# Output projection of the HGRN mixer as seven products on half matrices, product by product, with the operand sums on GpSimd

## The chip, the cores and the metric

The kernel runs on one core of one Trainium2 chip. The metric is device time in microseconds (us) of one execution, the median of repeated runs. A core has five engines that each work through their own instruction stream in order and wait for each other through semaphores: TensorE (PE: matrix multiplication; its weight loads are shown as PEld), VectorE (DVE), ScalarE (ACT), GpSimd (POOL) and SyncE (SP), which here does nothing but issue DMA transfers. GpSimd issues some DMA transfers too. A stream in order means that an instruction that waits holds up everything behind it on its engine.

## The reference

One layer of an encoder trunk over 1024 positions with a model width of 1024. Only the part around the changed product matters here:

```python
def _token_mixers(h, ...):
    proj = jnp.einsum("bsd,de->bse", h, w_in)
    glu_in, q, v, z_f, z_b, og, g_a, g_b = jnp.split(proj, SPLIT_POINTS, axis=-1)
    ...
    a = jax.nn.silu(_layernorm(a, ln_w, ln_b))
    a = jnp.einsum("bsc,cd->bsd", a, pw_w)
    o = _bi_hgrn2(q, v, z_f, z_b, lb[0], lb[1])
    ...
    bmix = (of * jax.nn.silu(og.astype(jnp.float32))).astype(h.dtype)
    bmix = jnp.einsum("bse,ed->bsd", bmix, o_w)
    return jax.nn.sigmoid(g_a) * a + jax.nn.sigmoid(g_b) * bmix
```

The line with `o_w` is the o projection: the 1024 x 1024 result of the eight heads (128 channels each) times a 1024 x 1024 weight. Its result is gated and added to the convolution branch, and the sum goes into `w_out`, the next product. After that comes the feed-forward part (`ffn_w_up`, `ffn_w_down`).

## The kernel before

Everything lies with channels on the 128 partitions and positions along the free axis, in two halves of 512 positions. A tile of 128 x 512 (called a page) is the unit of nearly all work. Every fp32 product is made of three matmuls (`mm3`, lines 149 to 151): weight and operand are each split into a rounded high part and a remainder (`split`, line 125: ScalarE casts the high part, then VectorE subtracts it from the source for the low part), and high x high, high x low and low x high are added up in PSUM. So one 128 x 128 block of weights against one half costs three 128x128 by 128x512 matmuls.

The stages run one after the other on TensorE: the input projections (those of large columns in pairs, `s_pairs`, by seven products on half matrices already); from about 362 to 470 us, in the midst of these pairs, the depthwise convolution's normalisation (`conv_norm`, a LayerNorm across partitions, from line 1086 on); the scan of the eight heads; the pointwise product of the convolution branch; the o projection from 867.7 us; `w_out` from 954.9 us; then the feed-forward part.

In `conv_norm`, TensorE has two small pieces of work for each half. `all_rows` (line 591) sums the four column tiles over partitions after the DVE line 1096, and `rstd_over_partitions` (line 602) does the same for the squares after the DVE line 1107. Both stand at fixed places between the matmuls of the projections, on TensorE's in-order stream. The DVE lines of the chain (1091, 1096, 1102, 1107) are pinned with `pin`, so they stay in program order with the other pinned rows.

A head's result is transposed at the end of its scan (line 1460), gated on DVE (line 1462) and stored to DRAM as `d_bm[h][half]`; head seven, the last, is split right away and stays in SBUF. `bm_loads(half)` loads the other seven heads of a half into pages `A` and splits them. The o projection itself is `o_jobs`: eight column tiles `i` of 128 output columns; for each, both halves; for each, eight heads `k`, three matmuls each: 8 x 2 x 8 x 3 = 384 matmuls. The weights come as eight loads of 512 KB (`raw_w`, two pages `wr`), each split into `wp` pages by ACT and DVE. `merge(i)` multiplies an accumulator with the gate `d_gb`, adds the convolution branch `d_a` (both loaded by SP) and splits the sum into the `mg` pages, the operands of `w_out`.

While the o projection runs, `weight_sums` (lines 1602 to 1620) prepares sums of the feed-forward part's first weights: 12 loads into eight pages called `h7`, 12 additions on DVE, 12 stores to `d_us`.

What sets the order: each engine's stream is in order. Tiles come from pools with a fixed number of pages (`ev` 3, `tm` 4, `wr` 2, `wp` 4, `h7` 8), and a page's next load waits for the last reader of its previous content. `Stream.fill(n)` emits n pieces of a product; `later(n, do)` puts a chore in a list that is run n pieces on. A scheduler orders unpinned instructions of different engines by what they depend on.

## Time and profile before

| | |
|---|---|
| median of 3 runs | 1706.88 us (1706.85 to 1707.17) |
| the profiled execution | 1706.98 us |
| its span on the core | 1705.0 us |
| PE busy | 1688.6 us (99%) |
| DVE busy | 1269.3 us (74%) |
| ACT busy | 827.3 us (49%) |
| POOL busy | 245.9 us (14%) |
| first matmul of the o projection / of `w_out` | 867.73 / 954.9 us |
| POOL busy from 860 to 955 us | 0 |
| DMA, mean over the span | 180 GB/s |

The span is what the profiler records between the first and the last instruction; 1.98 us of the profiled execution lie around it. Busy time of PE counts matmuls whose modelled ends overlap the next one, so the start-to-start distance is the honest price of a matmul. In rows of the trace, "out<-in" are tile names without buffer numbers, "x3" counts instructions, and a bracket at the end of a row tells how long the engine sat idle before it and what ended that.

### The profile page before, as it was taken

What the parts mean: (1) busy time and instruction counts of PE and PEld (TensorE: products, weight loads), DVE (VectorE), ACT (ScalarE), POOL (GpSimd) and SP (SyncE); (2) the same over time, 40 slices, a digit from 0 to 9 for tenths busy, and PEclk for the clock granted to TensorE, in tenths of its full rate; (3) what the DMA queues carried; (4) which work ended last, traced back from release to release, by engine and by line L of the source; (5) the groups of instructions that cost most, each with busy time, mean ns of one, the idle gap of its engine ahead of it and who ended that gap; (6) DMA issues with size and microseconds to landing.
All of it is one profiled execution on the core that took longest, in us unless ns stands there. A gap on an engine that the chain in (4) does not pass through costs nothing.

```text
span 1705.0 us, 30406 instructions
## 1 busy us (share of the span) xinstructions
PE 1688.6 (99%) x11719; PEld 1408.2 (83%) x11719; DVE 1269.3 (74%) x1938; ACT 827.3 (49%) x1562; POOL 245.9 (14%) x287
## 2 busy tenths in 40 slices
PE   9999999999999999999999999999999999999998
PEld 6788888888888888888888888888888888888787
DVE  5889899887678888888565467676777776657865
ACT  7454343335476777776432345444344434442334
POOL 1312222200001111111100003122222222000110
PEclk9999999999999999999999999999999999999999
DMA  7887887866573444436797455686777776773842
GB/s 240 284 213 186 191 196 172 205 187 206 165 236 100 139 129 134 129 116 221 241 294 243 128 167 176 153 171 143 172 164 178 164 183 149 237 260 102 212 98 99
DMA packets 332871, 306.17 MB, mean 180 GB/s; under 512 B 17454, under 2 KB 244918, under 8 KB 332726
## 3 DMA queue, kind: packets, MB, share of 16 engines
q1 hardware_dynamic: 285366, 265.42, 48.8%
q0 software_dynamic: 47360, 38.81, 15.4%
q8 instruction: 92, 1.51, 0.4%
q14 instruction: 53, 0.43, 0.1%
HBM read 201.40 MB, written 84.93 MB: 168 GB/s over the span
## 4 chain that ended last, share of the span: by engine, by line
PE 70%; ACT 1%; DVE 1%; DMA 0%; issue 0%; POOL 0%; POOLq 0%; ACTq 0%; DVEq 0%
PE mm L149 16%; PE mm L151 16%; PE mm L150 16%; PE sc L149 3%; PE sc L150 3%; PE sc L151 3%; PE ob L1433 2%; PE tr L149 2%; PE tr L150 2%; PE tr L151 2%; PE sc L1247 1%; PE sc L1333 1%; PE mm L1392 1%; PE sc L1392 1%; PE ob L1247 1%; PE tr L1382 0%
## 5 line engine op out<-in xcount | busy, mean ns | idle before, releaser
L149 PE MATMUL mm<-hx,wp 128*128 128x512 f32 x1068 | 425.7, 399 | 0.0
L151 PE MATMUL mm<-hx,wp 128*128 128x512 f32 x1068 | 417.0, 390 | 0.5 <-DVE wp L125 0.5
L150 PE MATMUL mm<-hx,wp 128*128 128x512 f32 x1068 | 416.2, 390 | 0.6 <-POOL hx L125 0.6
L125 ACT CAST wp<-wr 128x1024 fp32r<-128x1024 f32 (+2 forms) x146 | 146.9, 1006 | 224.3 <-PE mm L150 165.0
L151 PEld LDWEIGHTS mm<-hx,wp 128*128 128x128 f32 x1068 | 200.5, 188 | 44.6 <-DVE wp L125 1.6
L149 PEld LDWEIGHTS mm<-hx,wp 128*128 128x128 f32 x1068 | 200.6, 188 | 40.6 <-ACT wp L125 0.2
L150 PEld LDWEIGHTS mm<-hx,wp 128*128 128x128 f32 x1068 | 200.8, 188 | 39.9 <-POOL hx L125 1.0
L125 DVE TENSOR_TENSOR wp<-wr,wp 128x1024 fp32r<-128x1024 f32 (+2 forms) x144 | 169.5, 1177 | 39.8 <-ACT wp L125 39.4
L1065 DVE SCALAR_TENSOR_TENSOR acc<-gl,v_b,acc 128x1024 f32<-128x1024 f32 x120 | 153.5, 1280 | 1.7
L441 ACT COPY su<-mm 128x512 f32<-128x512 f32 x82 | 47.8, 583 | 84.4 <-PE mm L151 84.3
L1371 POOL DMA_DIRECT2D S<-D x64 | 36.1, 571 | 281.1 <-ACT jk L1438 125.3
L125 ACT CAST wq<-sw 128x1024 fp32r<-128x1024 f32 x41 | 43.2, 1054 | 61.3 <-PE mm L150 32.9
L1194 DVE TENSOR_TENSOR qF<-qF,tb 128x512 f32<-128x512 f32 x96 | 65.9, 686 | 9.5 <-ACT A L1228 8.9
L149 PE MATMUL tr<-hx,wp 128*128 128x512 f32 x180 | 70.1, 390 | 0.0
L151 PE MATMUL tr<-hx,wp 128*128 128x512 f32 x180 | 70.1, 389 | 0.0
L150 PE MATMUL tr<-hx,wp 128*128 128x512 f32 x180 | 70.0, 389 | 0.0
L1194 DVE TENSOR_TENSOR kG<-kG,tb 128x512 f32<-128x512 f32 x96 | 65.9, 687 | 4.0 <-ACT A L1228 2.2
L1710 DVE SCALAR_TENSOR_TENSOR tm<-gp,v_a,tm 128x512 f32<-128x512 f32 x88 | 66.0, 750 | 3.3 <-ACT tm L1708 1.3
L302 POOL DMA_DIRECT2D sw<-in_ffn_w_up_dram x38 | 49.8, 1502 | 116.0 <-DMA sw<-in_ffn_w_up_dram 72.4
L149 PE MATMUL sc<-hy,wq 128*128 128x512 f32 x164 | 63.9, 390 | 0.0
L151 PE MATMUL mm<-hy,wp 128*128 128x512 f32 x164 | 63.8, 389 | 0.0
L149 PE MATMUL mm<-hy,wp 128*128 128x512 f32 x164 | 63.8, 389 | 0.0
(377 smaller groups left out, 3721.9 us busy)
## 6 DMA issues: line engine op xcount, KB each, us to landing
wr<-in_w_in_dram SPq DMA_DIRECT2D x48, 512.0 KB, 5.6
wr<-in_ffn_w_up_dram SPq DMA_DIRECT2D x22, 512.0 KB, 5.6
sw<-in_w_in_dram SPq DMA_DIRECT2D x38, 256.0 KB, 3.1
d_g<-ft SPq DMA_DIRECT2D x38, 256.0 KB, 2.0
sw<-in_ffn_w_up_dram SPq DMA_DIRECT2D x38, 256.0 KB, 3.2
sw<-in_ffn_w_up_dram POOLq DMA_DIRECT2D x38, 256.0 KB, 6.7
wr<-sw POOLq DMA_DIRECT2D x32, 256.0 KB, 3.2
wr<-wr POOLq DMA_DIRECT2D x32, 256.0 KB, 3.3
```

Of the source, the lines that this page charges most:

```text
L125: parts = A.copy(hi, src), eng.tensor_tensor(lo, src, hi.bitcast(F32), op=ALU.subtract)
L149: T.matmul(acc, whi[:, k, :], ahi, start=first, stop=False, skip_group_check=again)
L150: T.matmul(acc, whi[:, k, :], alo, start=False, stop=False, skip_group_check=again)
L151: T.matmul(acc, wlo[:, k, :], ahi, start=False, stop=last, skip_group_check=again)
L302: G.dma_start(o, a, accum_op=ALU.add)
L441: A.copy(t, acc)
L1065: V.scalar_tensor_tensor(acc, g[:, k : k + S], tap(k), acc, op0=ALU.mult, op1=ALU.add)
L1194: return V.tensor_tensor(o, a, b, op=op)
L1247: T.matmul(b[g, o], A_t[:, at : at + 32], Q_t(at), start=True, stop=True)
L1371: G.dma_start(S_t[g : g + 32, :, g : g + 32], D_t[g : g + 32])
L1392: T.matmul(u[:, sl], kTs[d][:, sl], v[:, c, :], start=True, stop=True)
L1710: V.scalar_tensor_tensor(c, g[:, o + k : o + k + H], vec("fdw", k * NF + j), c, op0=ALU.mult, op1=ALU.add,)
```

## The change

The o projection becomes seven products on half matrices (Winograd's form of Strassen's scheme, as the input pairs do it). The output columns form four pairs `p` (column tiles `p` and `p + 4`), the heads form four pairs `k` (`k` and `k + 4`), and the positions their two halves. Seven products per pair `p`, four `k` each, three matmuls each: 7 x 4 x 4 x 3 = 336 matmuls. They go product by product over all pairs: 1 for p = 0 to 3, 2 for p = 0 to 3, 6 for p = 0 to 3, then 7 and 4 in turn for each p, then 5 and 3. Products 1, 2 and 4 use weights as they are, 7, 5, 6 and 3 use sums of weights; products 1, 2 and 3 use the heads' halves as they are, 7, 5, 6 and 4 use sums of them.

The sums of weights (`o_sums`) are made in the convolution's norm: eight chores of four loads, four DVE additions of 128x256 and a store to `d_os`, in pages `gl` of the convolution. The sums of operands (`operands`) are made between scan and product: 16 loads of `d_bm` into the eight `h7` pages, 12 additions on GpSimd for k = 0, 1, 2 and four on DVE for k = 3. Operand `b_o[2][3]`, which is half 0 of head seven, is split from the page `d_bm[7][0]` of k = 3; head seven goes through DRAM like the others. Four more loads (`later(28 + 2 * k, ...)`) serve product 3.

The merge multiplies by the gate on DVE (for products 2, 4 and 5 after an addition with a second accumulator, which ACT has copied to SBUF in some cases), and the convolution branch is then added by an accumulating DMA that GpSimd issues. The weights come in 14 groups of two products, 512 KB each. The feed-forward weights' sums are now emitted by the code of the stage behind, `s_out`.

```diff
-            if h == NH - 1:
-                bm[h][half] = split(hx(), hx(), bt, V)
-            else:
-                nc.sync.dma_start(d_bm[h][half], bt)
+            nc.sync.dma_start(d_bm[h][half], bt)
...
+    def o_sums(n):
+        p, ks = n // 2, slice(n % 2 * 2, n % 2 * 2 + 2)
+        t = gp0.tile([P, 4, 2, P], F32, tag="gl", name=nm("os"), bufs=NCW)
+        r, o = o_cols(p)
+        for q, (src, k0) in enumerate(((r, 0), (o, 0), (o, NK2), (r, NK2))):
+            nc.sync.dma_start(t[:, q], src[:, k0 + ks.start : k0 + ks.stop])
+
+        def add():
+            for a, b in ((0, 1), (1, 2), (2, 0), (3, 2)):
+                pin(V.tensor_tensor(t[:, a], t[:, a], t[:, b], op=ALU.add))
+            nc.sync.dma_start(d_os[p].rearrange("p q (k e) -> p q k e", e=P)[:, :, ks], t)
+
+        later(O_LATE, add)
...
     for half in range(2):
+        for n in range(half * ND // 2, half * ND // 2 + ND // 2):
+            later(1 + O_STEP * (n % (ND // 2)), lambda n=n: o_sums(n))
         for pieces in conv_norm(half):
             s_pairs.fill(pieces)
...
+    def merge(e, p, half, x0, x1=None, op=None):
+        i = p + e * NK2
+        t = next(gates_of)()
+        nc.sync.dma_start(t, d_gb[i][half])
+        if x1 is not None:
+            both = x0
+            if e + half < 2:
+                both = page(p4, "x2", 2)
+                A.copy(both, x0)
+            V.tensor_tensor(both, both, x1, op=op)
+            x0 = both
+        V.tensor_tensor(t, x0, t, op=ALU.mult)
+        G.dma_start(t, d_a[i][half], accum_op=ALU.add)
+        mg[i][half] = split(mg_page(), mg_page(), t, V)
...
+    def h7_page(src):
+        t = page(fw, "h7", 2 * NK2)
+        nc.sync.dma_start(t, src)
+        return t
...
+    def operands(k):
+        eng = V if k == NK2 - 1 else G
+        b11, b12, b22, b21 = [
+            h7_page(d_bm[k + h * NK2][half]) for h, half in ((0, 0), (0, 1), (1, 1), (1, 0))
+        ]
+        if k == NK2 - 1:
+            operand(2, k, b21)
+        for i, o, a, b, op in (
+            (7, b22, b12, b22, ALU.subtract),
+            (5, b12, b11, b12, ALU.subtract),
+            (6, b11, b22, b11, ALU.subtract),
+            (4, b21, b11, b21, ALU.add),
+        ):
+            eng.tensor_tensor(o, a, b, op=op)
+            operand(i, k, o)
...
+    o_items = [(i, p) for i in (1, 2, 6) for p in range(NK2)]
+    o_items += [(i, p) for p in range(NK2) for i in (7, 4)]
+    o_items += [(i, p) for i in (5, 3) for p in range(NK2)]
+    o_groups = [o_items[n : n + 2] for n in range(0, len(o_items), 2)]
...
+    for n, d in enumerate(d_us):
+        later(5, weight_sums(*up_cols(n), ND // 2, d))
+        s_out.fill(5)
```

Three places show how instructions move. The same code has higher line numbers in the changed kernel (line 1107 becomes 1129, 602 becomes 610, 149 to 151 become 150 to 152, 125 becomes 126).

The first place is SyncE's stream (SP) at the end of the scan, where the o projection's loads begin. Before, these rows stand there (`d_a` are stores of the convolution branch, `tm` and `ev` the merge's loads, `wr` weights of the o projection, `h7` feed-forward weights):

```order
L1157 DMA d_a_6_1_153<-ev_1703_10533 128x512
L1157 DMA d_a_7_1_155<-ev_1705_10550 128x512
L1575 DMA tm_1762_10780<-d_a_1_1_143 128x512
L1575 DMA ev_1741_10657<-d_gb_0_0_172 128x512
L136 DMA wr_1765_10789<-in_hgrn_o_w_dram 128x8x128
L1608 DMA h7_1746_10692<-in_ffn_w_up_dram 128x4x128
```

In the changed kernel the stream has the store of head seven's second half, the last store of `d_a`, and then 16 loads of `d_bm` into the eight `h7` pages; shown are the first three, the eighth, and the last two with the row behind them:

```order
L1487 DMA d_bm_7_1_283<-ev_1713_10640 128x512
L1181 DMA d_a_7_1_155<-ev_1711_10631 128x512
L1613 DMA h7_1730_10666<-d_bm_0_0_268 128x512
L1613 DMA h7_1731_10668<-d_bm_0_1_269 128x512
L1613 DMA h7_1732_10670<-d_bm_4_1_277 128x512
...
L1613 DMA h7_1741_10696<-d_bm_5_0_278 128x512
...
L1613 DMA h7_1756_10742<-d_bm_7_1_283 128x512
L1613 DMA h7_1757_10744<-d_bm_7_0_282 128x512
L1663 DMA wr_1771_10783<-in_hgrn_o_w_dram 128x4x128
```

The load of `d_bm_7_0` is the sixteenth of the sixteen, and its page is the one that `h7_1741` had, the eighth: with eight pages, the sixteenth load takes the eighth page again.

The second place is TensorE's and DVE's o projection. On TensorE the first tile of product 2 (`tr_1782`) ends with the operand `hx_1758`, `hx_1759`, which is the high and the low part of that page; they are the operands of the twentieth group of three matmuls of the projection (sixteen of product 1, then the fourth of product 2):

```order
L150 MATMUL tr_1782_10852<-hx_1703_10585,wp_1774_10812 128x512
L151 MATMUL tr_1782_10852<-hx_1704_10586,wp_1774_10812 128x512
L152 MATMUL tr_1782_10852<-hx_1703_10585,wp_1775_10813 128x512
L150 MATMUL tr_1782_10852<-hx_1758_10746,wp_1774_10812 128x512
L151 MATMUL tr_1782_10852<-hx_1759_10747,wp_1774_10812 128x512
L152 MATMUL tr_1782_10852<-hx_1758_10746,wp_1775_10813 128x512
L150 MATMUL ob_1787_10876<-hx_1697_10573,wp_1774_10812 128x512
```

Before, TensorE went on through all eight heads of one column tile, and no `h7` page was an operand; this is the head of that row of matmuls:

```order
L1460 MATMUL tr_1727_10596<-ident_68,tm_1649_10337 128x128 x4
L149 MATMUL mm_1740_10632<-hx_1677_10465,wp_1732_10616 128x512
L150 MATMUL mm_1740_10632<-hx_1678_10466,wp_1732_10616 128x512
L151 MATMUL mm_1740_10632<-hx_1677_10465,wp_1733_10617 128x512
L149 MATMUL mm_1740_10632<-hx_1680_10471,wp_1732_10616 128x512
```

On GpSimd the twelve sums stand in one row; the last of the first eight writes `h7_1741`, and the split of it on DVE (`mg_1717`) is its last reader. What moved: the operand of the first tile of product 2 now hangs on a page behind eight sums.

The third place is DVE in the convolution's norm, first half, ahead of the third line 1107 (after which TensorE's line 602 runs). Before:

```order
L1107 TENSOR_TENSOR tm_567_3682<-tm_567_3682,tm_568_3691 128x512
L1107 TENSOR_TENSOR tm_567_3682<-tm_567_3682,tm_570_3702 128x512
L828 TENSOR_TENSOR ev_573_3729<-su_572_3713,mm_548_3609 128x512
L1107 TENSOR_TENSOR tm_567_3682<-tm_567_3682,tm_571_3711 128x512
L125 TENSOR_TENSOR wq_562_3662<-sw_556_3647,wq_561_3661 128x1024
L828 TENSOR_TENSOR ev_581_3769<-sc_550_3611,su_569_3693 128x512
```

In the changed kernel (line 1107 is 1129, 828 is 836, `os` are the pages of `o_sums`):

```order
L836 TENSOR_TENSOR ev_577_3768<-su_576_3752,mm_550_3628 128x512
L1129 TENSOR_TENSOR tm_570_3711<-tm_570_3711,tm_574_3741 128x512
L126 TENSOR_TENSOR wq_565_3691<-sw_559_3676,wq_564_3690 128x1024
L1094 TENSOR_TENSOR os_571_3719<-os_571_3719 128x256
L836 TENSOR_TENSOR ev_585_3813<-sc_552_3630,su_573_3727 128x512
L126 TENSOR_TENSOR wq_568_3698<-w4_563_3688,wq_568_3698 128x512
L1094 TENSOR_TENSOR os_571_3719<-os_571_3719 128x256 x3
L1129 TENSOR_TENSOR tm_570_3711<-tm_570_3711,tm_575_3750 128x512
```

The third line 1129 now stands behind the row of line 836 that reads the accumulator `sc_552`, a split and the additions of line 1094. In the second half it stands, in the same way, behind a split, four additions and two rows of line 299 (298 before); before, the split alone stood between it and the second line 1107, one of the two rows of line 298 stood further ahead and the other behind it.

105 lines of the change are left out of this document (73 added, 32 removed).

## The prediction

> **What bounds the kernel now.** I read the page's first part, then the busy time by stretches, then the timeline of each engine around the places that the change touches.
>
> ```profile
> PE 1688.6 (99%) x11719; PEld 1408.2 (83%) x11719; DVE 1269.3 (74%) x1938; ACT 827.3 (49%) x1562; POOL 245.9 (14%) x287
> ```
>
> TensorE has 16.4 us without work in 1705.0 us. So a matmul that goes away is worth its full pitch, and a wait that TensorE does not have now is paid in full. The stage of the o projection, by stretches (PE, PEld, DVE, ACT and POOL busy, then the granted clock, the DMA share and GB/s):
>
> ```profile
> 870.00:880.00 10.00, 10.00 (x46) 8.29 (x45) 7.00 (x11) 1.77 (x4) 0.00 (x0) 1.00 0.98 305
> 880.00:900.00 20.00, 20.00 (x90) 16.57 (x89) 15.09 (x22) 4.49 (x6) 0.00 (x0) 1.00 0.92 300
> 920.00:940.00 20.00, 20.00 (x90) 16.53 (x89) 9.46 (x13) 3.97 (x5) 0.00 (x0) 1.00 0.61 195
> ```
>
> TensorE never waits here, at the full clock. DVE is busy for three quarters of the time at first, ScalarE for a fifth, GpSimd for nothing, and the DMA engines are nearly full. So GpSimd has room for sums, and what can hurt is a latency: something that arrives late at TensorE's in-order stream.
>
> **What the matmuls are worth.** The pitch is read from the product behind, where 384 matmuls follow each other without a gap:
>
> ```profile
> L149 PE MATMUL mm<-mg,wp x128: 389/389/389, 954.9 to 1041.3; 128*128 128x512 f32 x128
> L151 PE MATMUL mm<-mg,wp x128: 389/389/389, 955.4 to 1041.8; 128*128 128x512 f32 x128
> ```
>
> From the first start (954.9) to the last (1041.8) are 383 steps in 86.9 us, 0.2269 us each (the 389 ns overlap). The change takes 384 matmuls to 336: 48 x 0.2269 = **10.9 us less**, 0.64%.
>
> **The wait at the second product.** TensorE's rows before and at the start of the projection:
>
> ```profile
> 867.38 0.60 PE L1460 MATMUL tr<-ident,tm 128*128 128x128 f32 x4
> 867.73 0.49 PE L149 MATMUL mm<-hx,wp 128*128 128x512 f32 x1
> ```
>
> TensorE's stream up to there is unchanged, so product 1 begins at 867.73 again. Its 48 matmuls take 10.9 us, to 878.6; nine matmuls on, at 880.7, comes the first that reads half 0 of head seven. Before, that operand was split from SBUF right after the gating. Now it is the sixteenth load of the sixteen, into the page of the eighth. I follow that chain.
>
> When the loads begin: SP issues them behind the last store of `d_a`, and that waits for DVE's last merge. Before:
>
> ```profile
> 868.15 1.37 DVE L1156 TENSOR_TENSOR ev<-mm,ev 128x512 f32<-128x512 f32 x2
> 870.04 0.74 DVE L1462 SCALAR_TENSOR_TENSOR ev<-tr,v_a,og 128x512 f32<-128x512 f32 x1
> 871.30 1.22 DVE L125 TENSOR_TENSOR wp<-wr,wp 128x1024 fp32r<-128x1024 f32 x1
> 851.21 0.90 SPq L1507 DMA_DIRECT2D A<-d_bm  x2
> ```
>
> DVE now does here a merge (0.6 us from start to start), a 1024-wide split (1.14, from its 1.22), the gating (0.66) and the last merge (0.69): 868.15 + 3.1 = 871.2. One issue of SP is 0.45 us (0.90 for two), so the first load goes at 871.6 and the third, which completes the first sum's pair, at 872.5.
>
> How long a load takes to land, by the closest rows (KB, then us):
>
> ```profile
> A<-d_bm SPq DMA_DIRECT2D x14, 256.0 KB, 4.5
> ev<-d_gb SPq DMA_DIRECT2D x16, 256.0 KB, 2.6
> tm<-d_a SPq DMA_DIRECT2D x16, 256.0 KB, 6.6
> ```
>
> Same source, size and queue is 4.5; 2.6 is the lower bound, 6.6 the upper one (that wait was in a full queue). With 4.5 the first sum starts at 877.0, with 2.6 at 875.1.
>
> The sums on GpSimd. The trace has one f32 128x512 operation with two inputs in SBUF and nothing beside it, and eight while DVE works:
>
> ```profile
> L1784 POOL TENSOR_TENSOR tm<-tm,xq 128x512 f32<-128x512 f32 x1 | 1.3, 1287 | 0.0
> L125 POOL TENSOR_TENSOR hx<-ev,hx x8: 1301/1454/2280, 42.6 to 64.0; 128x512 fp32r<-128x512 f32 x8
> ```
>
> Eight sums take 10.3 us by the first and 11.6 by the median of the second; I take 11.0. They end at 885.4 at the earliest, at about 888.0 by my values. Then comes the split of the eighth sum, whose last reader frees the page:
>
> ```profile
> L125 ACT CAST mg<-tm 128x512 fp32r<-128x512 f32 x16 | 9.9, 622 | 52.0 <-DVE tm L1577 52.0
> L1577 DVE TENSOR_TENSOR tm<-tm,ev 128x512 f32<-128x512 f32 x16 | 11.1, 692 | 0.5
> ```
>
> ScalarE 0.62 and DVE 0.69 make 1.3 us: 889.3 (earliest 886.7). SP has only waited meanwhile, and with it all that stands behind (weights of products 2 and 6, gates), so the DMA queue has run empty; the sixteenth load then lands after 2.6 to 4.5 us, and I take 3.8. The cast of the high part is 0.62 more. TensorE goes on at 893.7 (earliest 889.9, latest by these rows 895.2, or 897.3 with the first landing at 6.6), against 880.7. The low part comes 0.69 behind, against one matmul of 0.23, another 0.46 us if the next matmul waits. **A stall of about 13 us**, between 9.3 and 17. It is longer than what the 48 matmuls save. The lost time moves every later deadline by as much, which is why I cost the remaining splits (28 operands instead of 16, 14 groups of weights instead of 8) at nothing: DVE's quarter and ScalarE's four fifths of free time and the stall hide them; without that cover each DVE row of 0.69 would stand on the path.
>
> DMA behind the stall: SP still issues about 60 transfers of 256 KB up to the last weights, and GpSimd 12 accumulating ones, some 19 MB. At the 300 GB/s of the row above that is 63 us; from 889.3 the last would land at 952, and the last group of weights, with its split of 2.3 us (1.22 on DVE, a cast ahead), is wanted at about 949 (867.73 + 312 matmuls + 13 us, less 2.3). So the queue is at its limit: between nothing and 5 us late, I take 1. The end of the projection waits for the last merge: multiplication 0.69, issue and landing of an accumulating transfer, cast 0.62:
>
> ```profile
> xr<-d_x POOLq DMA_DIRECT2D x16, 256.0 KB, 4.4
> L1890 POOL DMA_DIRECT2D xr<-d_x x16 | 13.8, 862 | 193.0 <-DVE xr L1887 191.6 <-ACT wq L125 1.4
> ```
>
> 0.69 + 0.86 + 4.4 + 0.62 = 6.6 us; `w_out` needs this operand after its first half (24 matmuls) and nine more, 7.5 us on. It is covered, by 0.9 us; I take 0, and 2 us as the upper end.
>
> **The waits in the convolution's norm.** The 32 additions are 128x256. DVE has rows near that size: 416 ns with PSUM, 692 ns for twice the size:
>
> ```profile
> L1954 DVE TENSOR_TENSOR xr<-mm,xr 128x256 f32<-128x256 f32 x16 | 6.6, 416 | 0.9 <-PE mm L151 0.9
> ...
> sum 99.00, PE 98.44 PEld 81.30 DVE 66.29 ACT 48.88 POOL 2.57; mean PE 24.61 PEld 20.32 DVE 16.57 ACT 12.22 POOL 0.64
> ```
>
> The second row sums the stretches from 371 to 470 us. I take 0.34 us start to start for an addition. That is 11 us on a DVE that is busy for 66 of these 99 us, so the sum fits; the places decide. First half: the row of line 828 reads an accumulator that TensorE finishes just ahead of line 602, so whatever stands between it and the third line 1107 is time in which TensorE stands.
>
> ```profile
> 395.08 0.39 PE L151 MATMUL sc<-hx,wq 128*128 128x512 f32 x1
> 395.31 0.94 PE L602 MATMUL ob<-ones_r,tm 128*128 128x1 f32 x8
> ...
> 392.85 0.69 DVE L828 TENSOR_TENSOR ev<-su,mm 128x512 f32<-128x512 f32 x1 [1.83 <-PE mm L151]
> 393.45 0.68 DVE L1107 TENSOR_TENSOR tm<-tm,tm 128x512 f32<-128x512 f32 x1
> 395.51 0.69 DVE L828 TENSOR_TENSOR ev<-sc,su 128x512 f32<-128x512 f32 x1 [0.24 <-PE sc L151]
> 396.16 0.69 DVE L125 TENSOR_TENSOR wq<-w,wq 128x512 fp32r<-128x512 f32 x1
> ```
>
> Before, the third line 1107 was done at 394.1. Now: 396.77 (end of the split's 0.61) + 3 x 0.34 + 0.68 = 398.5. TensorE could go on at 395.31: **3.2 us**. Second half:
>
> ```profile
> 443.75 0.69 DVE L828 TENSOR_TENSOR ev<-tr,su 128x512 f32<-128x512 f32 x1 [1.52 <-issue]
> ...
> 444.95 1.22 DVE L125 TENSOR_TENSOR wp<-wr,wp 128x1024 fp32r<-128x1024 f32 x1
> 446.09 0.68 DVE L1107 TENSOR_TENSOR tm<-tm,tm 128x512 f32<-128x512 f32 x1
> ...
> 447.57 0.95 PE L602 MATMUL ob<-ones_r,tm 128*128 128x1 f32 x8
> ```
>
> Between the split (ended at 446.09) and line 1107 now stand four additions (1.36), a row of 1024 (1.14) and one of 512 (0.6): 449.2 + 0.68 = 449.9, **2.3 us** behind 447.57. Together 5.5. At least 4 if the additions cost 0.27 and fill DVE's pauses better; up to 8 where the four more loads ahead on SP (4 x 0.45 = 1.8 us) make a weight page late before line 591 as well. Loads and stores of `o_sums` are otherwise SP's idle time.
>
> **The sum**, against the profiled execution's 1706.98 us (0.1 above the median of the runs): 1706.98 - 10.9 + 13.0 + 1.0 + 5.5 = 1715.6; less 0.1 for the median, **1715.5 us**. With the lower ends 1706.9 - 10.9 + 9.3 + 4 = 1709.3; with the upper ones (17, 5, 2 and 8) 1728.
>
> **Rivals.**
>
> *The saving stands, the head comes in time.* Then 1706.9 - 10.9 + 5.5 = 1701.5, and 1696.0 if the norm's waits are hidden too; faster. The point from which it decides: the sixteenth load would have to be issued by 875.6 (880.7 - 0.62 - 4.5), that is, without waiting for the eighth page. For it: the code splits this operand ahead of its own k's sums, and GpSimd was idle. Against it: the row of loads, and that eight sums cannot take under 10.3 us by any row. Some overlap that I don't see would be needed. Chance 0.13.
>
> *Only the head waits.* The norm's chain finds DVE's pauses, and the queue keeps up: 1706.9 - 10.9 + 13.0 = 1709.0, or with the short stall 1706. No change that can be told. For it: DVE sat idle for 1.83 us ahead of 392.85 and 1.52 ahead of 443.75. Against it: the pauses end with the very rows that the third line 1107 stands behind. Chance 0.22.
>
> *TensorE comes back slow after the stall.* The start of the trace shows it at half its rate after idleness:
>
> ```profile
> 2.32 0.24 PE L502 MATMUL mm<-ident,vr 8*128 8x8 f32 x1 [2.32 <-DMA vr<-in_attn_norm_w_dram]
> ...
> 6.76 0.42 PE L667 MATMUL tr<-ident,xt 128*128 128x128 f32 x1
> 6.97 0.37 PE L667 MATMUL ob<-ident,xt 128*128 128x128 f32 x1
> ...
> 8.39 0.27 PE L667 MATMUL tr<-ident,xt 128*128 128x128 f32 x1
> 8.50 0.27 PE L667 MATMUL sc<-ident,xt 128*128 128x128 f32 x1
> ```
>
> At 6.8 us these transposes start every 0.21 us, from 8.39 on every 0.11. TensorE began at 2.32, so it was slow for 6 us at most and lost up to 3 us. A stall of 13 us might bring that state back, and GpSimd's sums might be longer beside it (the row of eight above has 2.28 as its longest): 1715.5 + 1.5 to 3, and up to 3 more, is 1717 to 1722. After the start this trace has no long stand of TensorE (16.4 us of idleness in all), so it can't be weighed from here. Chance 0.15.
>
> The Trainium skill, "TensorE: Matmul & The Clock Gate", Part 1 (The HAM clock gate), says that the array's clock is halved after an idle window of about 3.4 us and released after about as long of sustained work. By that rule a stall of this length would cost some 1.7 us more (an estimate from that page), 1717.2. The rows at the start agree with a slow beginning; how long a later one lasts no row here shows, and the forecast leaves it out.
>
> **How the numbers follow.** The forecast has 0.5, the rivals 0.13, 0.22 and 0.15. The predicted time is the forecast's. Its own range is 1710 to 1722; down to 1703 it takes in the second rival and part of the first. I give 1703 to 1722: some 0.10 are left out below, 0.07 above. A measurement of this kernel tells some 0.2%, 3.4 us, from no change. Faster than 1703.5: 0.14; within: 0.23; slower than 1710.3: 0.63.
>
> **What would show it.** In the trace after: 336 matmuls between the scan's last transposes and `w_out`; TensorE idle once for 9 to 17 us about nine matmuls into product 2, released by ScalarE's cast of an `h7` page loaded from `d_bm`; GpSimd with sums of 1.3 to 1.5 us from about 876 on; SP silent from about 879 to 889; TensorE idle for 3 us ahead of line 610 (602 before) near 395 us and for 2 us near 450. Wrong would be: a second product without a gap (the chain is covered, and the time is near 1701), a gap in the norm's first half under 1 us, or gaps at later weights (the DMA queue is the bound, and the sum too low).

## The result and the profile after

The changed kernel takes 1758.16 us, the median of four runs (1755.41 to 1759.66), the kernel before 1707.03: a ratio of 1.0298, with a 95% interval of 1.028 to 1.0316. That is 51 us slower where 8.6 were forecast. The profiled execution took 1759.66 us, with a span of 1757.9.

The first line of the page after:

```profile
PE 1696.7 (97%) x11671; PEld 1407.7 (80%) x11671; DVE 1303.5 (74%) x1988; ACT 847.6 (48%) x1592; POOL 278.7 (16%) x315
```

TensorE has 61.2 us without work in its span, 44.8 more than before. And it is busy for 8.1 us longer although 48 matmuls, 10.9 us, are gone: so the rest took 19.0 us more. 44.8 + 19.0 - 10.9 = 52.9, which is the difference of the two spans. The loss has two parts of different kinds, waits and slow work. What TensorE waits for (us in total, times, longest):

```profile
PE tr L150 <- ACT hx L126: 17.5, 1, 17.5
PE ob L610 <- DVE tm L1129: 8.3, 2, 4.8
PE tr L150 <- ACT xq L1689: 8.2, 2, 7.6
PE mm L150 <- ACT mg L126: 4.1, 3, 2.1
...
PE tr L152 <- DVE wp L126: 1.6, 1, 1.6
PE ob L150 <- ACT xq L1689: 1.4, 2, 0.7
```

The first is the stall at product 2, the second the norm's two waits. The others, 15.3 us, lie behind the stall: at products 7 and 4, where a copy frees their bank late, and at the start of `w_out`. None of them was there before. The same stage by stretches (PE, PEld, DVE, ACT and POOL busy, granted clock, DMA share, GB/s); everything lies 14.6 us later, since the norm costs that much:

```profile
880.00:900.00 20.00, 15.51 (x71) 12.48 (x69) 11.29 (x11) 4.80 (x7) 7.31 (x5) 1.00 0.75 254
900.00:910.00 10.00, 0.00 (x0) 0.00 (x0) 9.18 (x7) 3.71 (x6) 9.61 (x7) 0.52 0.52 175
910.00:920.00 10.00, 5.63 (x12) 4.09 (x13) 9.69 (x14) 6.08 (x10) 1.73 (x2) 0.50 0.72 216
```

Between 900 and 910 us DVE and GpSimd are full and TensorE is empty. Then the granted clock is 0.50. TensorE's rows there:

```profile
895.12 0.39 PE L152 MATMUL tr<-hx,wp 128*128 128x512 f32 x1
913.03 0.80 PE L150 MATMUL tr<-hx,wp 128*128 128x512 f32 x1 [17.52 <-ACT hx L126]
915.17 0.79 PE L151 MATMUL tr<-hx,wp 128*128 128x512 f32 x1 [1.34 <-DVE hx L126]
915.76 0.63 PE L152 MATMUL tr<-hx,wp 128*128 128x512 f32 x1
916.18 0.63 PE L150 MATMUL ob<-hx,wp 128*128 128x512 f32 x1
...
920.88 0.43 PE L152 MATMUL ob<-hx,wp 128*128 128x512 f32 x1
921.14 0.39 PE L150 MATMUL tr<-hx,wp 128*128 128x512 f32 x1
```

The stall is where it was forecast, after nine matmuls of product 2, with the releaser that was forecast. Behind it the matmuls start every 0.427 us (915.76, 916.18) until 920.88, and every 0.227 from 921.14 on. This happens five times: after 399, 459, 913, 963 and 1009 us, each time for 5 to 8 us. About 17 of the 19.0 us lie in these five stretches; the rest stands next to shorter waits. The two feeders of the stall, first GpSimd:

```profile
892.45 19.35 POOL L1635 TENSOR_TENSOR h<-h,h 128x512 f32<-128x512 f32 x12 [21.76 <-issue]
```

and DVE:

```profile
902.48 1.53 DVE L126 TENSOR_TENSOR mg<-h,mg 128x512 fp32r<-128x512 f32 x1
904.15 1.53 DVE L126 TENSOR_TENSOR hx<-h,hx 128x512 fp32r<-128x512 f32 x1
...
912.49 0.69 DVE L126 TENSOR_TENSOR mg<-h,mg 128x512 fp32r<-128x512 f32 x1
```

A sum takes 1.61 us on average, and DVE's splits, which follow the sums one for one every 1.67 us, take 1.53 instead of 0.69 each; when GpSimd stops (912) they take 0.69 again. The first sum of the row, with nothing beside it, took 1.30. One after the other a sum and a split would take 1.30 + 0.69 = 1.99 us, so working side by side saves only 0.3 us a pair.

### The profile page after: what moved, and what is told of

It is laid out like the page before. It is cut to its first block, busy times and chain, and to the rows that moved or that the text cites. A ratio compares the mean times of both kernels' runs of the same rounds, so it can differ in the third digit from the quotient of the medians.

```text
span 1757.9 us, 30563 instructions
## 1 busy us (share of the span) xinstructions
PE 1696.7 (97%) x11671; PEld 1407.7 (80%) x11671; DVE 1303.5 (74%) x1988; ACT 847.6 (48%) x1592; POOL 278.7 (16%) x315
## 5 line engine op out<-in xcount | busy, mean ns | idle before, releaser
L150 PE MATMUL mm<-hx,wp 128*128 128x512 f32 x976 | 391.1, 401 | 0.6 <-ACT wp L126 0.6
L152 PE MATMUL mm<-hx,wp 128*128 128x512 f32 x976 | 382.0, 391 | 1.3 <-DVE wp L126 1.3
L151 PE MATMUL mm<-hx,wp 128*128 128x512 f32 x976 | 381.3, 391 | 0.6 <-POOL hx L126 0.6
L126 ACT CAST wp<-wr 128x1024 fp32r<-128x1024 f32 (+2 forms) x152 | 153.2, 1008 | 230.2 <-PE mm L151 164.7
L152 PEld LDWEIGHTS mm<-hx,wp 128*128 128x128 f32 x976 | 183.7, 188 | 42.2 <-DVE wp L126 2.6
L126 DVE TENSOR_TENSOR wp<-wr,wp 128x1024 fp32r<-128x1024 f32 (+2 forms) x150 | 176.9, 1179 | 53.3 <-ACT wp L126 53.0
L150 PEld LDWEIGHTS mm<-hx,wp 128*128 128x128 f32 x976 | 183.9, 188 | 38.2 <-ACT wp L126 1.2
L151 PEld LDWEIGHTS mm<-hx,wp 128*128 128x128 f32 x976 | 184.1, 189 | 36.6 <-POOL hx L126 1.1
L150 PE MATMUL tr<-hx,wp 128*128 128x512 f32 x200 | 78.3, 392 | 17.5 <-ACT hx L126 17.5
L152 PE MATMUL tr<-hx,wp 128*128 128x512 f32 x200 | 78.2, 391 | 1.6 <-DVE wp L126 1.6
L151 PE MATMUL tr<-hx,wp 128*128 128x512 f32 x200 | 78.2, 391 | 1.3 <-DVE hx L126 1.3
L150 PE MATMUL sc<-hy,wq 128*128 128x512 f32 x164 | 64.4, 393 | 0.0
L151 PE MATMUL sc<-hy,wq 128*128 128x512 f32 x164 | 64.3, 392 | 0.0
L152 PE MATMUL sc<-hy,wq 128*128 128x512 f32 x164 | 64.3, 392 | 0.0
```

Of the source, the lines that this page charges most:

```text
L126: parts = A.copy(hi, src), eng.tensor_tensor(lo, src, hi.bitcast(F32), op=ALU.subtract)
L150: T.matmul(acc, whi[:, k, :], ahi, start=first, stop=False, skip_group_check=again)
L151: T.matmul(acc, whi[:, k, :], alo, start=False, stop=False, skip_group_check=again)
L152: T.matmul(acc, wlo[:, k, :], ahi, start=False, stop=last, skip_group_check=again)
```

## The experiments

All times are beside runs of the kernel before on the same chip (1707.0 to 1707.8 us). Where one time stands, it is one profiled execution; six runs at the end were timed in five rounds. The changed kernel's own four executions lie 4.3 us apart, so a single time within about 4 us of its 1758.16 says little by itself, and the rows of the trace have to decide.

**Do the losses of the two places add up?** The theory (A) is that norm and projection lose apart from each other, each by its waits and the slow work behind them. First the kernel before with only the sums of weights added, whose result nothing reads:

```diff
+        for n in range(half * ND // 2, half * ND // 2 + ND // 2):
+            later(1 + O_STEP * (n % (ND // 2)), lambda n=n: o_sums(n))
```

> The kernel before, with the weights' sums of the o projection added to the convolution's norm (loads, 32 additions, stores; nothing reads them). Theory A (two waits of TensorE ahead of line 610, 3.4 and 4.8 us in the trace after, and each followed by a stretch at half the matmul rate): 1707 + 14.5 = about 1721.5 us, with two waits and two slow stretches. Theory B (as predicted: the two waits alone, 5.5 us; the slow rows come from elsewhere): about 1712.5 us, no slow stretch.

Measured: 1721.44, 14.1 us more. It waits for 9.6 us, at the same two places (line 604 is 610 of the changed kernel):

```profile
PE ob L604 <- DVE tm L1126: 9.6, 2, 6.2
```

The other 4.5 us are slow work behind them. The counterpart is the changed kernel without the sums, its products 7, 5, 6 and 3 on plain columns of the weights:

```diff
-            later(1 + O_STEP * (n % (ND // 2)), lambda n=n: o_sums(n))
...
-        return d_os[p][:, (7, 5, 6, 3).index(i)].rearrange("p (k e) -> p k e", e=P)
+        return (r, o)[i % 2][:, :NK2]
```

> The changed kernel without the weights' sums; products 7, 5, 6 and 3 read plain columns of the weights in their place, so the o projection's result is another one. Theory A (the costs of the two stages add up): 1758.2 - 14.5 = about 1743.7 us, and the o projection still has its wait of 17.5 us. Rival (the loads of the sums, with longer rows, or the shift in time, weigh in the o projection): off by more than 3 us either way.

Measured: 1743.29, 36.0 us more than before. 14.1 + 36.0 is 50.1 of the 51: within the noise the places add up.

**Does TensorE's idleness alone make the slow work?** Dummy matmuls on TensorE fill the norm's two waits:

```diff
+        for _ in range(busy):
+            T.matmul(b, ones_r, h_std(0, 0)[0], start=True, stop=True)
```

> The changed kernel with 13 and 19 useless 128x128 by 128x512 matmuls on TensorE ahead of line 610 in the two halves of the norm, which overwrite columns that nobody reads. 32 matmuls more. Theory A (a wait of over 3 us drops the rate, and busy time in its place keeps it): the same time from the scratch accumulator to line 610, no slow stretch behind, so about 7 us less: 1751 us. Theory B (the slow stretch has nothing to do with idleness): 1758 us or a little more, slow stretches as before.

Measured: 1754.8. The stretches where the changed kernel's TensorE worked for 6.55 us (390 to 400) and 5.16 us (450 to 460), in this kernel (the columns as above):

```profile
390.00:400.00 10.00, 9.71 (x43) 7.63 (x41) 9.83 (x19) 4.17 (x7) 0.00 (x0) 1.00 0.50 160
400.00:410.00 10.00, 9.90 (x47) 8.33 (x48) 3.46 (x7) 5.33 (x14) 1.23 (x2) 1.00 0.57 178
450.00:460.00 10.00, 10.00 (x49) 8.35 (x48) 5.93 (x11) 1.11 (x4) 1.20 (x2) 1.00 0.73 232
460.00:470.00 10.00, 9.39 (x41) 7.41 (x41) 4.52 (x7) 6.36 (x15) 0.00 (x0) 1.00 0.39 131
```

Nothing of the chain was made faster; TensorE only had something to do, and the clock stayed at 1.00. TensorE reached the stall of product 2 5.2 us earlier. So the slow work comes from TensorE's own idleness and not from what DVE does. The wait at product 2 became 18.1 us, which gives 0.5 back, and the span is 4.9 us shorter (1753.0 against 1757.9). The forecast of 1751 was missed by 4; the total, one execution, lies just below the fastest of the changed kernel (1755.41), so the evidence is the norm's own rows.

**Where do the norm's waits come from?** The same additions on GpSimd:

```diff
-                pin(V.tensor_tensor(t[:, a], t[:, a], t[:, b], op=ALU.add))
+                pin(G.tensor_tensor(t[:, a], t[:, a], t[:, b], op=ALU.add))
```

> The changed kernel with the weights' sums of the norm on GpSimd instead of DVE. Theory A (TensorE's two waits there come from the additions that stand ahead of the third line 1129 on DVE's stream): both waits fall under 1 us and no slow stretch follows, 1758.2 - 14.5 + 0 to 3 = 1744 to 1747 us. Rival (GpSimd and DVE hinder each other, as beside the operand sums, where a DVE row took 1.53 instead of 0.69 us): the norm's chain gets longer and waits of 2 to 4 us stay, 1752 to 1758 us.

Measured: 1759.47; nothing is won, and the time lies a little above the rival's range. The norm's first wait goes and the second grows to 5.9 us; another comes, of 4.21 us for DVE's line 836. DVE's timeline beside GpSimd's additions, from 436 us on, in this kernel:

```profile
441.32 1.75 DVE L126 TENSOR_TENSOR wq<-sw,wq 128x1024 fp32r<-128x1024 f32 x1
...
446.59 1.70 DVE L126 TENSOR_TENSOR wp<-wr,wp 128x1024 fp32r<-128x1024 f32 x1
448.21 1.22 DVE L1129 TENSOR_TENSOR tm<-tm,tm 128x512 f32<-128x512 f32 x1
```

These shapes take 1.22, 1.22 and 0.68 in the changed kernel. Then the additions stay on DVE but start fourteen pieces of work later, behind the norm's chain:

```diff
-            later(1 + O_STEP * (n % (ND // 2)), lambda n=n: o_sums(n))
+            later(15 + 4 * (n % (ND // 2)), lambda n=n: o_sums(n))
```

> The changed kernel with the weights' sums begun 14 pieces later in each half of the norm, so that on DVE's stream all their additions stand behind the third line 1129. Theory A (the place on the in-order stream costs the time, not the work): both waits in the norm under 0.5 us, no slow stretch, 1758.2 - 14.5 = about 1743.7 us, at most 1746. Rival (11 us of additions and 12 MB of transfers are too much for this stage anywhere): 1750 us or more.

Measured: 1744.51. Both waits and both slow stretches of the norm are gone; a wait of 0.88 us is new. So it is the place of the additions in DVE's row, not their amount.

**The stall at product 2.** Head seven's half 0 in a page of its own, loaded first:

```diff
-        if k == NK2 - 1:
-            operand(2, k, b21)
...
+    t = tmp()
+    nc.sync.dma_start(t, d_bm[NH - 1][0])
+    operand(2, NK2 - 1, t)
```

> The changed kernel with half 0 of head seven loaded ahead of the 16 loads into a page of its own, one load more. Theory A (that operand waits for the eighth page): the wait of 17.5 us at the fourth group of product 2 is gone; the next operand that hangs on the sums is product 6's, k = 3, wanted at about 906 and there at about 915, so a wait of 8 to 10 us stands there, and the time is about 1750 us. Rival (the wait is set by GpSimd's sums as a whole or by the DMA queue): the wait stays at product 2, 1757 to 1760 us.

Measured: 1766.65, a miss. The wait is longer, and it is another one (TensorE's timeline, product 2):

```profile
915.64 0.79 PE L150 MATMUL tr<-hx,wp 128*128 128x512 f32 x1 [20.73 <-ACT wp L126]
```

Product 2's weights are late instead, since their load stands on SP behind the same loads of `d_bm` (it is issued at 907.95) and their cast on ScalarE behind the operands' casts (it starts at 914.54). So the page was only the last link; the whole in-order chain behind it is late. With sixteen pages (eight of the later `mg` pages lent), head seven first:

```diff
+        if k < 2:
+            return h7_page(src)
+        t = raws.pop(0).bitcast(F32)
+        nc.sync.dma_start(t, src)
```

> The changed kernel with 16 pages for the operands' 16 loads (eight of them pages that the merge uses later) and half 0 of head seven loaded first; the sums stay on GpSimd. Theory A (SP's stream stands still for 20 us on pages, and the weights of product 2 behind it too): the wait at product 2 is gone or below 3 us; GpSimd's sums at 1.67 us each are late for product 6 instead (the eleventh at about 911 against 905), a wait of 5 to 10 us; 1742 to 1750 us. Rival (the DMA queue is full at that place): the wait at product 2 stays above 10 us.

Measured: 1753.22, above the 1742 to 1750 of the theory. TensorE still waits for product 2's weights, 9.5 us, and for product 6, 6.1. The same with all the operands' sums on DVE, product 6's operands first:

```diff
-            eng.tensor_tensor(o, a, b, op=op)
-            operand(i, k, o)
+            V.tensor_tensor(o, a, b, op=op)
+            if i == 6:
+                operand(i, k, o)
+            else:
+                behind.append((i, k, o))
```

> As the one with 16 pages, but with the operands' sums on DVE, and product 6's operands first. Theory A (GpSimd and DVE share the way to SBUF, a sum and a split together take 1.67 us): sums and splits at 0.6 us each, product 6's operands ready at about 903, its wait gone; waits left at weights and merges; 1733 to 1742 us. Rival (GpSimd's sums were hidden work, and DVE becomes the bound): no better than the one with GpSimd, 1745 us or more.

Measured: 1748.32, a miss as well (the theory had 1733 to 1742); 6.8 us for product 2's weights and several of 2 to 4 us behind. The two steps with sixteen pages were right in their direction and too small, since the next thing in the same queues was late as well.

**The waits behind the stall.** In the changed kernel the wait of 7.56 us for a copy (line 1689) stands behind a cast on ScalarE that waits for an accumulating DMA, and that was issued by GpSimd late (its timeline):

```profile
955.34 0.85 POOL L1605 DMA_DIRECT2D tm<-d_a  x1 [19.99 <-DVE tm L1604]
```

GpSimd waited 20 us for DVE's multiplication, and DVE stood at a row of the feed-forward sums, whose load was late (DVE's timeline):

```profile
951.41 0.69 DVE L1724 TENSOR_TENSOR h<-h,h 128x512 f32<-128x512 f32 x1 [7.69 <-DMA h<-in_ffn_w_up_dram]
```

A first try to hold these sums back tied their loads to a row of DVE:

```diff
+        with tc.issue_after(merged[0].ins):
+            sums = weight_sums(*up_cols(n), ND // 2, d)
```

> The changed kernel with the loads of the feed-forward weights' sums held back until the last merge. Theory A (DVE stood 7.7 us at such a sum for its load, which made a merge, the casts behind it on ScalarE and the copy of product 7 late): the wait of 7.6 us near 963 and its slow stretch go, and the waits at the start of the next product with them: 8 to 16 us less, 1742 to 1750 us. Rival (the merge's accumulating transfers are late by themselves): 1755 to 1760 us with the wait in place.

Measured: 1758.02. It held nothing, since such an edge orders only instructions of one engine; the question stayed open. So the loads were held on SP behind the last weights' load, and the additions on DVE behind the last merge:

```diff
+        with tc.issue_after(loaded[0].ins):
+            sums = weight_sums(*up_cols(n), ND // 2, d)
...
+            with tc.issue_after(merged[0].ins):
+                sums()
```

> The changed kernel with the feed-forward weights' sums held back on both streams: their loads behind the last weights of the o projection on SP, their additions behind the last merge on DVE. (The earlier kernel named a DVE row for the loads, which holds nothing on SP.) Theory A (DVE stood 7.7 us at such an addition for its load, and the merge, the casts and the copy of product 7 came late by it): the wait of 7.6 us near 963 and its slow stretch are gone, 8 to 14 us less, 1744 to 1750 us. Rival (the accumulating transfers are what is late): still a wait of 5 us or more there, 1754 to 1760 us.

Measured: 1750.3; the wait of 7.6 is 1.0 now. And with the merge's addition on DVE, its operand loaded by SP, instead of the accumulating DMA:

```diff
-        G.dma_start(t, d_a[i][half], accum_op=ALU.add)
-        mg[i][half] = split(mg_page(), mg_page(), t, V)
+        V.tensor_tensor(a, a, t, op=ALU.add)
+        mg[i][half] = split(mg_page(), mg_page(), a, V)
```

> The changed kernel with the convolution branch loaded by SP and added on DVE in the merge, as before the change, in place of GpSimd's accumulating transfer. Theory A (a cast on ScalarE waits 5 to 9 us for the transfer, and the copy of product 7 and the operands of the next product behind it): the waits of 7.6 us near 963 and of 1.7 and 2.2 us near 1010 fall to under 2 us together, 8 to 15 us less, 1743 to 1750 us. Rival (the transfers are late because DVE and the DMA queue are): waits of 5 us or more stay near 963, 1754 us or more.

Measured: 1740.4. That wait is 1.2, those at the start of `w_out` are gone, and only the slow stretches of the norm and of the stall are left. Sixteen more additions on DVE are cheaper than sixteen transfers in the chain.

**All together.** Late sums in the norm, sixteen pages with head seven first, the weights of products 1 and 2 ahead of the loads, all sums on DVE with product 6 first, merges on DVE, the feed-forward sums held:

```diff
+    s_o.fill(1)
+    last21 = raw_page(NK2 - 1, d_bm[NH - 1][0])
+    operand(2, NK2 - 1, last21)
+    s_o.fill(8)
...
     for k in range(NK2):
         operands(k)
```

> The changed kernel with all causes taken away that the runs point to: the norm's sums later, 16 pages for the operands' loads and head seven first, the weights of products 1 and 2 ahead of them, the operands' sums on DVE with product 6's first, the merge's addition on DVE, the feed-forward sums held back. Theory A (the stalls and the slow stretches behind them are all that was lost): TensorE waits less than 6 us in the projection, and the time is 1707 - 10.9 + 0 to 12 = 1696 to 1708 us. Rival (the stage is bound by DVE or the DMA queue with the added work): 1712 us or more.

Measured: 1720.86, in the rival's range. The big stall is gone, but product 6 waits (TensorE's waits in this kernel):

```profile
PE mm L152 <- DVE wp L126: 6.1, 3, 4.6
PE mm L150 <- ACT hx L126: 3.5, 1, 3.5
PE mm L150 <- DVE x L1605: 3.4, 1, 3.4
```

and DVE, the third number of each row, has no pause there:

```profile
890.00:900.00 10.00, 5.69 (x17) 3.13 (x16) 10.00 (x16) 6.12 (x11) 0.00 (x0) 0.81 0.91 320
900.00:910.00 10.00, 5.34 (x16) 3.57 (x15) 10.00 (x18) 6.13 (x12) 0.00 (x0) 0.84 0.16 48
```

So either DVE's load is a floor, or its order is wrong. The remaining runs, timed in five rounds each, decide that; no work is taken out in any of them (DVE has 2016 rows in each, as here). First the rows of product 6 ahead of all others, and products 7 and 4 interleaved by pair, so that the copy between them is hidden. (In this run product 5's sums have the opposite sign, so its result differs.)

```diff
+    with tc.issue_after(o_splits[5].ins):
+        for k in range(NK2):
+            operand(7, k, halves[k][2])
...
-    o_items += [(i, p) for p in range(NK2) for i in (7, 4)]
+    o_items += [(7, 0), (7, 1), (4, 0), (7, 2), (4, 1), (7, 3), (4, 2), (4, 3)]
```

> The combined version of the run before (1720.9) with its order on VectorE mended: the sums of product 6 in pages of their own and ahead of all else, the operands of products 7, 4 and 5 and product 2's merges behind the split of product 6's second group of weights, product 2's copies in other pages, and products 7 and 4 interleaved by pair. Theory (what is left over there is order alone, waits at product 6 and the slow stretches behind them): of its waits 3.5, 3.4, 4.6 and 4 x 0.7 us most goes, and the slow stretches of about 5 us with them: 1701 to 1708. Rival (VectorE, busy 10.0 of 10 us from 890 to 910 there, has more work in products 2 and 6 than TensorE gives it time for, so that a wait only changes its place): 1715 to 1721.

Measured: 1711.63, ratio 1.0029 (1.0018 to 1.0039), a little above the range of the order theory and well below the rival's. About 3 us of waits were left at product 6, and one of 3.44 us for the split of product 7's first weights behind product 2's merges. That row moved ahead:

```diff
+    s_o.fill(4)
+    with tc.issue_after(o_splits[6].ins):
         for b11, b12, b22, b21, t6 in halves.values():
             V.tensor_tensor(b21, t6, b21, op=ALU.add)
```

> The version before with three orders more mended: of VectorE, the split of product 7's first weights ahead of product 2's merges (it was late there by 3.44 us) and nothing between product 6's sum and split of the last pair; of SP, the loads that only product 4 needs behind those of product 6. Theory (order alone): the wait of 3.44 us goes with its slow stretch of 1.6 us, and of the 3.3 us at product 6 about half goes: 1711.6 - 5.0 - 2 = 1704 to 1706, at or a little below the kernel before. Rival (VectorE has too much to do up to 925 us): a wait of 2 to 4 us appears at product 7 or 4 instead, 1709 to 1712.

Measured: 1712.22, ratio 1.003 (1.0019 to 1.004): the rival's number. The wait is gone and one of 5.38 us at product 4 has come. But in DVE's timeline there is a pause ahead of the row that all others were held behind:

```profile
902.48 1.23 DVE L1686 TENSOR_TENSOR wp<-wr,wp 128x1024 fp32r<-128x1024 f32 x1 [3.65 <-ACT wp L1685]
```

A pause of 3.65 us in DVE ahead of the new wait speaks for the order rather than for the floor. Two of product 2's merges and product 5's sums moved further back:

```diff
+        for do in rest[:2]:
+            do()
+    s_o.fill(4)
+    with tc.issue_after(o_splits[8].ins):
+        for do in rest[2:]:
+            do()
```

> The version before with the rows that now stood ahead of the weights moved once more: the last two of product 2's merges behind the split of the weights' group that holds product 4's second pair, product 5's operands behind the next group's, and SP's loads of the operands of pairs 2 and 3 ahead of product 6's second group of weights. Theory (order alone): the wait of 5.38 us at product 4 goes with its slow stretch of 1.6, and of the 2.5 us at product 6 at least 1: 1712.2 - 7.0 - 1 to 2.5 = 1702.7 to 1704.2, below the kernel before. Rival (VectorE has no room before 930 us): the wait appears at a third place, 1709 to 1713.

Measured: 1707.71, ratio 1.0003 (0.9994 to 1.0012), between the two theories. The 5.38 is gone; five waits of 0.5 to 2.0 us are left. The later merges behind the next weights' split:

```diff
+            with tc.issue_after(o_splits[g + 1].ins):
+                for args in todo:
+                    merge_rest(*args)
```

> The version before with the merges' multiplies and adds of products 4, 5 and 3 put behind the split of the weights' group that follows on VectorE, and product 3's operand splits later. Theory (order alone): of its five waits in this stage (0.52, 1.18, 1.99, 0.77, 1.47 us) and a slow stretch of 1.4 us, the 1.99, the slow stretch and the 0.77 go: 1707.7 - 4.2 = 1703.5, faster than the kernel before by 0.2%. Rival (VectorE is full there; what is put back comes due a little later): the waits move, 1706 to 1709, no difference from the kernel before.

Measured: 1712.57, ratio 1.0029 (1.0018 to 1.0041), slower than either theory had. All waits of the stage behind product 6 are gone, and one stands at the next stage's first weights (TensorE's timeline):

```profile
958.06 0.79 PE L152 MATMUL mm<-mg,wp 128*128 128x512 f32 x1 [6.78 <-DVE wp L126]
```

Their cast on ScalarE was done at 949.6, their split on DVE came at 956.8, behind eleven rows of merges. It went ahead of them:

```diff
+    s_out.fill(1)
+    with tc.issue_after(o_splits["out"].ins):
+        for args in tail[:]:
+            merge_rest(*args)
```

> The version before, where every wait but 2.2 us at product 6 had gone from the stage and one of 6.78 us stood at the first weights of the product that follows (w_out): its split was VectorE's eleventh row behind ScalarE's cast, behind product 3's merges. Here only product 3's first multiply stays ahead of it; the splits of product 5's last two merges and the rest of product 3's come behind it. Theory (order alone): 6.8 us and the slow stretch of 1.4 us go, and up to 1 us comes back as a short wait there: 1712.6 - 8.2 + 0 to 1 = 1704.4 to 1705.4, a little below the kernel before (ratio 0.998 to 0.999). Rival (VectorE's load is a floor that moves the wait on): the second half of the first w_out product waits for product 3's last merges, 1707 to 1710.

Measured: 1707.58, ratio 1.0004 (0.9995 to 1.0013): the rival's number, and its place too. The wait is five short ones now, in the second half of the first `w_out` product, and TensorE is slow behind them (its timeline):

```profile
959.15 0.50 PE L151 MATMUL mm<-mg,wp 128*128 128x512 f32 x1 [0.65 <-DVE mg L126]
...
960.61 0.72 PE L150 MATMUL mm<-mg,wp 128*128 128x512 f32 x1 [0.72 <-ACT mg L126]
961.80 0.80 PE L151 MATMUL mm<-mg,wp 128*128 128x512 f32 x1 [0.47 <-DVE mg L126]
962.40 0.63 PE L152 MATMUL mm<-mg,wp 128*128 128x512 f32 x1
...
967.52 0.42 PE L152 MATMUL mm<-mg,wp 128*128 128x512 f32 x1
```

Last, the first two `w_out` products run half by half, which gives the merges 5.4 us, and product 6's operands go ahead of product 2's additions:

```diff
+            for half in range(2):
+                for (_, r), wi in zip(both, w):
+                    yield from r(wi, (half,))
...
+            with tc.issue_after(o_splits["t" if p < 2 else "b"].ins) if p and e == 0 else nullcontext():
+                V.tensor_tensor(both, both, x1, op=op)
```

> The version before, level with the kernel before, had two groups of short waits left, each with a slow stretch behind it: 0.52 and 1.18 us at product 6, slow to 898.8, and 0.65, 0.72 and 0.47 us in the first w_out product, slow for 6 us. Here the sums and splits of product 6's last pairs go ahead of product 2's merges on VectorE, and the first two w_out products run half by half, so that product 3's merges have 5.4 us more. Theory (order alone): 3.5 us of waits go, and with them 21 matmuls at half rate, 4.2 us: 1707.6 - 7.7 = 1700 to 1703, faster than the kernel before by 0.3 to 0.4%. Rival (VectorE's load is the floor): short waits come back in w_out or product 7, 1705 to 1709.

Measured: 1702.79 (eight runs, 1701.25 to 1707.0), ratio 0.9978 (0.9967 to 0.9988): 4.7 us faster than the kernel before, 55 faster than the change, as the order theory had it. The first line of the page of its profiled execution (1701.48 us), and its stage by stretches:

```profile
PE 1679.6 (99%) x11671; PEld 1399.0 (82%) x11671; DVE 1308.5 (77%) x2016; ACT 845.7 (50%) x1592; POOL 246.1 (14%) x287
```

```profile
880.00:900.00 20.00, 19.67 (x86) 15.64 (x86) 18.35 (x27) 10.29 (x16) 0.00 (x0) 1.00 0.88 311
920.00:940.00 20.00, 19.45 (x83) 15.12 (x82) 20.00 (x31) 8.99 (x14) 0.00 (x0) 1.00 0.71 225
```

DVE is busy for 38.35 of these 40 us and TensorE for 39.12, at the full clock. So DVE's load was no floor at 1720.9 us: the same number of rows fits in less time. The order made the difference. It was not DVE's alone: products 7 and 4 interleaved on TensorE, `w_out` half by half, SP's loads in another order and two more pages for copies came with it, and were not tried one by one. Of the 10.9 us, TensorE's busy time shows 9.0 (1688.6 to 1679.6), and 3.7 went back as idle time (20.1 against 16.4).

## Why the prediction was wrong

**The saving** (48 matmuls, 10.9 us) holds: the last version shows 9.0 of it in busy time. **The stall at product 2** was right in place, chain and releaser, and mis-sized: 13 us forecast, 17.5 and 1.3 measured. From the first load on, the links were forecast at 5.4 (first sum's start), 11.0 (eight sums), 1.3 (split), 3.8 (last load) and 0.62 (cast); measured are 6.5, 12.7, 2.2, 5.0 and 0.61. (The latest end in the forecast, 895.2, adds up to 895.0 by its own terms; nothing hangs on it.) The sum's price came from a row with nothing beside it and from a median beside light work on DVE; here DVE's splits followed the sums one for one, and each slowed the other.

**The norm** was forecast at 3.2 and 2.3 us, and waits for 3.4 and 4.8. The first is the chain as worked out. In the second a row that stood ahead of the fourth addition waited for a transfer, which the sum had not asked for:

```profile
456.66 1.23 DVE L299 TENSOR_TENSOR sw<-sw,sw 128x1024 f32<-128x1024 f32 x1 [2.33 <-DMA sw<-in_w_in_dram]
457.80 0.42 DVE L1094 TENSOR_TENSOR os<-os 128x256 f32<-128x256 f32 x1
458.13 0.68 DVE L299 TENSOR_TENSOR wr<-wr,sw 128x512 f32<-128x512 f32 x1
458.74 0.68 DVE L1129 TENSOR_TENSOR tm<-tm,tm 128x512 f32<-128x512 f32 x1
```

**The step that failed most in its reasoning** is "which is why I cost the remaining splits ... at nothing", with 1 us for the DMA queue and 0 for the last merge. The argument was that a stall moves all later deadlines. But what feeds them stands in in-order streams of its own: SP issued nothing else for 21.8 us (its timeline in the changed kernel, below), GpSimd issued the merges' transfers behind DVE's multiplications, and DVE stood for the feed-forward sums. 15.3 us of waits came behind the stall. h3_hold2 and h4_merge_dve each took one link away, which gave back 8 and 18 us while the stall stayed (17.1 and 17.7 us). So most of these waits come from the merges' chain itself; how much the stall adds to them is not shown.

```profile
885.93 21.77 SPq L1613 DMA_DIRECT2D h<-d_bm  x16
```

**The half rate** is the largest term that was left out: most of the 19.0 us of longer busy time (about 17 in the five stretches), where the forecast had none and the rival one stretch of 1.5 to 3 us, at 0.15. The rival's mechanism was right. At the stall it cost 2.8 us (fourteen steps, from the start at 915.17 to the one at 921.14, take 5.97 us, at full pitch 3.18), but every other wait of 3.4 us and more paid it again, the norm's two as well, and so did two shorter ones, of 1.67 and 2.15 us, near 1009. In e3_keep_busy it went without any faster chain. The rule cited with the prediction (the Trainium skill, "TensorE: Matmul & The Clock Gate", Part 1 (The HAM clock gate)) halves the clock after an idle window of about 3.4 us. The trace agrees for the waits of 3.44 and more; it was to be applied to all of them, not to the stall alone. It does not cover the stretch near 1009, nor h10_best5, where one wait of 1.99 us was enough, nor h12_best7, where TensorE was slow for 6 us behind waits of 0.65, 0.72 and 0.47; there the measurement decides.

What the traces do fit is a count over fixed steps. The granted clock changes between 1.00 and 0.50 only on a grid of 3.41 us, and it goes with how busy TensorE was in the whole step before, not with the length of a single wait. In the norm's first stretch of the changed kernel (columns as above: behind the comma PE's busy time, the clock third from the end):

```profile
395.28:398.69 3.41, 0.43 (x2) 0.01 (x1) 3.34 (x8) 0.62 (x1) 0.00 (x0) 1.00 0.39 113
398.69:402.10 3.41, 2.94 (x11) 2.75 (x12) 1.71 (x3) 0.00 (x0) 0.56 (x2) 0.50 1.10 369
...
405.52:408.93 3.41, 3.41 (x16) 2.80 (x16) 1.23 (x1) 2.83 (x7) 0.00 (x0) 1.00 0.00 0
```

In h12_best7 a step with 1.77 us of work was followed by a slow one (first two rows), in h13_best8 a step with 1.90 was not (last two rows):

```profile
957.30:960.71 3.41, 1.77 (x6) 0.59 (x5) 3.30 (x6) 1.37 (x3) 0.00 (x0) 1.00 0.96 301
960.71:964.13 3.42, 2.95 (x7) 1.96 (x8) 3.06 (x6) 1.73 (x3) 0.00 (x0) 0.50 0.92 272
972.55:975.97 3.42, 1.90 (x9) 1.24 (x7) 3.02 (x5) 0.00 (x0) 0.00 (x0) 1.00 1.01 364
975.97:979.38 3.41, 3.17 (x14) 2.64 (x15) 2.69 (x5) 2.45 (x4) 0.00 (x0) 1.00 0.96 344
```

In all twenty traces of this case a full-clock step in which TensorE was busy for less than 0.43 of the time was followed by a slow one, and a step of more than 0.53 never; between the two both occur.

So the terms stand, by the two profiled spans (52.9 us apart): saving -10.9; stall 18.8 for 13; norm 8.3 for 5.5; behind the stall 15.3 for 1; longer busy time, most of it the half rate, 19.0 for 0; 2.4 in small waits. The rival that the saving stands was excluded for the kernel as written, and shown possible by h13_best8 with another order. Left open: what the stall's removal alone is worth, since each of the three tries (e4_own_page, f2_pages, f3_pages_dve) moved the wait to the next thing in the same queues.

## What to carry to other kernels

Where TensorE is at 99%, fewer matmuls pay only if nothing that feeds them comes late, and a wait of some us costs up to the double, for the slow work behind it. A stall gives no cover to work that waits in the same in-order queue (the weights in e4_own_page): follow each queue past the blocked instruction. And when a busy engine makes others wait, first look for rows that could stand later in its stream: from 1720.9 to 1702.8 us, DVE did the same number of rows, and the order changed, mostly its own.

## What the runs showed of the hardware

- TensorE starts 128x512 matmuls every 0.427 us instead of 0.227, at a granted clock of 0.50, after a step of a fixed 3.41 us grid in which it was busy for less than 0.43 of the time (in some cases up to 0.53), and for one step or more (6.83, 10.24 and 20.48 us in the changed kernel). A wait of 3.4 us and more did it in every case here, but so did one of 1.99 us (h10_best5) and 0.65, 0.72 and 0.47 us within 3.5 us (h12_best7), while single waits of 1.76 (h13_best8) and 1.90 us (h3_hold2) did not.
- GpSimd and DVE on f32 operands in SBUF slow each other: a 128x512 sum on GpSimd takes 1.61 us beside DVE's splits (1.29 alone), the split 1.53 instead of 0.69, the 1024-wide split 1.7 instead of 1.22. A sum and a split together take 1.67 us; DVE alone does two such rows in 1.2 (0.69 each, 0.6 from start to start, from 913 us on in the changed kernel). The 1024-wide rows are those of f1_conv_pool.
